# A prologue with the latent first, constant matmuls between TensorE's waits, and a second norm put in other places

## The chip, the cores and the metric

The kernel runs on one core of a Trainium2 chip. The metric is the time of one execution on the device in microseconds (us). A core has TensorE (PE, matrix products; PEld is its loading of stationary operands), VectorE (DVE), ScalarE (ACT), GpSimd (POOL) and SyncE (SP, which issues DMAs here). Each engine works through its own list of instructions in order and waits on semaphores for the others.

## The reference, cut to what matters

One layer: two token mixers (a gated linear recurrence over the sequence and a gated MLP over chunks) on a normed and modulated input, then a GEGLU MLP with a 3x3 depthwise convolution. The latent `x` has 512 tokens, the context `ctx` 256, both with 1024 channels. All arithmetic is float32.

```python
def _modulate(x, g, shift, scale):
    return _rmsnorm(x, g) * (1.0 + scale) + shift
m_x = (silu(c) @ w_mod + b_mod).reshape(B, 6, 1, D)      # for the latent
m_c = (silu(c_ctx) @ w_mod + b_mod).reshape(6, D)        # for the context
hc = _modulate(ctx, g_norm1, m_c[0], m_c[1])
pc = hc @ w_in[:, :W_R]                                  # the context needs only the columns rx
...                                                      # conv and recurrence of the context: end states
hx = _modulate(x, g_norm1, m_x[:, 0], m_x[:, 1])
px = hx @ w_in                                           # columns rx, rg, u, v, gr, gg
...                                                      # recurrence from those states, gating, merge
x = x + m_x[:, 2] * (merged @ w_out)
h2 = _modulate(x, g_norm2, m_x[:, 3], m_x[:, 4])
x = x + m_x[:, 5] * _conv_ffn(h2, w_up, ...)
return _rmsnorm(x, g_final)
```

## The kernel before, in words

Activations lie channel-major: 8 tiles of 128 channels (index k) by tokens. A float32 product is made of three passes in a rounded format: operand and weight are each split into a high part (`wh`, `hxh`: an ACT copy) and the rest (`wl`, `hxl`: a DVE subtraction), and high x high, high x low and low x high are summed in PSUM (`mm3`, L139 to L141). `Weights` (L50 to L103) hands out weight blocks in program order: `load` issues the DMA into `raw` (two buffers) on SP's queue, `prepare` splits a block, `take` returns it after preparing some blocks ahead.

The **prologue** (L214 to L350) starts every chain. In order: `c_row` and the modulation weights `wm` of block 0 are loaded, then the latent in 8 pieces, then further `wm`, the weight blocks `w_first` and the context. `sig` is silu of both conditioning rows; a transpose (`psc`) turns them into columns `c32`. `mod_cols(k)` makes shift and scale of channel block k: 16 small matmuls in four row strips into `pm`, an ACT copy `mrow`, one matmul that turns the rows into columns (`pm<-sel,mrow`), and two DVE operations into `ms`. `norm_of` squares the 8 latent blocks on ACT (L281, L284), adds them one after another on DVE (`sqs`, L285), sums over partitions with matmuls against ones (`pss`, L289), takes square root and reciprocal (`rstd_of`, L196, L197), and spreads the result over partitions (`spread_rows`, `rb`, L203). `mod_h(k, n)` applies norm and modulation to block k of the latent or the context (L328 to L330) and splits it. Then `products` (L317) multiplies block k of latent and context with six column tiles of `w_in` (rx, rg, gr) and two for the context (`rxc`); eight k-steps accumulate in PSUM. `mod_cols` and `mod_h` run two blocks ahead (`LEAD = 2`).

In the **heads** after it, `rx_head` multiplies the next rx columns while DVE makes the convolution of the head before (`pad`, `cacc`, `xr`, `xrh`, `xrl`), and `gates_head` needs its `xrl`.

Around the **second norm** (L646 to L733) the merged tokens are multiplied with `w_out`: five channel blocks over all tokens, the last three (5 to 7) in two token halves (`out_half`). `out_post` adds the residual (`x1c`, L672), squares and sums (`osq`, L677, L678). `norm2(half)` makes the statistics of one half (`qss`, `qrb`, L684 and L203) and turns its eight blocks into `h2h` and `h2l` (L694 to L697). Then the first four blocks of `w_up` (`FIRST`) run over the first half (`up_half`), blocks k 0 to 3, then `norm2` of the second half, then the rest. The two splits `wl` of each of the first two `w_up` units are made on GpSimd; two of the four pairs have buffers of their own (`extra`).

A scheduler sets each engine's order from the program, the dependencies and priorities; `after(a, b)` adds an order without a wait.

## Time and profile before

| | us |
|---|---|
| runs before, median (lowest to highest of 3) | 967.9 (967.74 to 967.97) |
| the profiled execution | 967.45 |
| its span, first to last instruction | 965.7 |
| PE busy | 938.9 (97%) |
| DVE, ACT, POOL busy | 642.5 (67%), 470.0 (49%), 41.8 (4%) |

The profiled execution lasts 1.8 us longer than its span. In the page's row of 40 slices (24.1 us each) PE reads 3 in the first slice, 8 or 9 in all others but the last, which reads 7. PE is the engine to follow: in the chain of work that ended last it has 87%. Times below count from the first instruction. A float32 matmul outside the three-pass scheme stands in the trace as two records, so 4 instructions are "x8".

### The profile page before, as it was taken

To read this page: it belongs to the slowest core of one execution; us is meant where nothing else is said; L and a number is where in the kernel's file an instruction comes from. 1 tells how busy PE (TensorE), PEld (TensorE's weight loads), DVE (VectorE), ACT (ScalarE), POOL (GpSimd) and SP (SyncE) were. 2 spreads that over 40 slices of the span, in tenths; PEclk is the share of its full clock that TensorE was granted. 3 is DMA by queue.
4 is the path that set the end of the run, shared out by engine and by line. 5 is a ranking of instruction groups with operands and counts; after the bars stand their busy time and mean duration, and the time that the engine had idled before them with its cause. 6 is when DMAs were issued, how large, how long until landed. Compare 5 with 4: busy or idle time off the path is not lost.

```text
span 965.7 us, 11855 instructions
## 1 busy us (share of the span) xinstructions
PE 938.9 (97%) x4787; PEld 791.0 (82%) x4787; DVE 642.5 (67%) x863; ACT 470.0 (49%) x639; POOL 41.8 (4%) x69
## 2 busy tenths in 40 slices
PE   3999999999999999999999998999999999999997
PEld 3788888888888788888888888988888888888886
DVE  3667595969493886555773547598885437788644
ACT  4536969794989681233332334254333122333323
POOL 0000000000000011000200112000000000000020
PEclk9999999999999999999999999999999999999999
DMA  9542122122131266622853531122212232222222
GB/s 354 213 163 88 44 88 75 57 88 94 61 114 61 85 224 239 235 88 88 315 212 121 203 126 49 61 97 98 94 66 88 101 140 87 88 88 88 88 88 88
DMA packets 23511, 116.85 MB, mean 121 GB/s; under 512 B 2576, under 2 KB 3744, under 8 KB 14368
## 3 DMA queue, kind: packets, MB, share of 16 engines
q1 hardware_dynamic: 17488, 94.59, 27.3%
q0 software_dynamic: 5968, 21.50, 6.2%
q8 instruction: 37, 0.61, 0.3%
q14 instruction: 18, 0.15, 0.0%
HBM read 113.98 MB, written 2.10 MB: 120 GB/s over the span
## 4 chain that ended last, share of the span: by engine, by line
PE 87%; DVE 5%; ACT 5%; issue 1%; DMA 1%; SPq 0%; DVEq 0%; ACTq 0%
PE up L139 8%; PE up L141 8%; PE up L140 8%; PE d L140 4%; PE d L141 4%; PE d L139 4%; PE pr L139 2%; PE pr L140 2%; PE pr L141 2%; PE u L139 2%; PE u L140 2%; PE u L141 2%; PE gg L140 2%; PE pg L139 2%; PE gg L139 2%; PE pg L140 2%
## 5 line engine op out<-in xcount | busy, mean ns | idle before, releaser
L93 ACT CAST wh<-raw 128x1024 fp32r<-128x1024 f32 (+1 forms) x156 | 161.9, 1040 | 299.9 <-PE up L140 79.6
L95 DVE TENSOR_TENSOR wl<-raw,wh 128x1024 fp32r<-128x1024 f32 (+1 forms) x152 | 184.2, 1214 | 153.0 <-ACT wh L93 136.1
L139 PE MATMUL up<-h2h,wh 128*128 128x512 f32 (+1 forms) x384 | 143.8, 374 | 0.0
L141 PE MATMUL up<-h2h,wl 128*128 128x512 f32 (+1 forms) x384 | 143.5, 374 | 0.0
L140 PE MATMUL up<-h2l,wh 128*128 128x512 f32 (+1 forms) x384 | 143.2, 373 | 0.0
L792 DVE SCALAR_TENSOR_TENSOR acc<-up,sm,acc 128x441 f32<-128x441 f32 (+2 forms) x176 | 120.2, 693 | 14.2 <-ACT acc L785 10.4
L141 PEld LDWEIGHTS up<-h2h,wl 128*128 128x128 f32 x384 | 73.0, 190 | 12.4
L139 PEld LDWEIGHTS up<-h2h,wh 128*128 128x128 f32 x384 | 73.0, 190 | 12.3
L140 PEld LDWEIGHTS up<-h2l,wh 128*128 128x128 f32 x384 | 73.0, 190 | 12.3
L140 PE MATMUL d<-wl,fh 128*128 128x512 f32 (+1 forms) x186 | 70.3, 378 | 0.0
L139 PE MATMUL d<-wh,fh 128*128 128x512 f32 (+1 forms) x186 | 70.3, 378 | 0.0
L141 PE MATMUL d<-wh,fl 128*128 128x512 f32 (+1 forms) x186 | 70.3, 378 | 0.0
L795 ACT ACTIVATE acc<-acc 128x512 f32<-128x512 f32 x22 | 13.9, 632 | 61.4 <-DVE acc L792 61.4
L558 DVE SCALAR_TENSOR_TENSOR wmod<-wmod,cbx 128x1024 f32<-128x1024 f32 x24 | 29.3, 1223 | 17.7 <-DMA wmod<-in_w_mod 17.7
L139 PEld LDWEIGHTS d<-wh,fh 128*128 128x128 f32 x186 | 35.0, 188 | 6.6
L140 PEld LDWEIGHTS d<-wl,fh 128*128 128x128 f32 x186 | 35.0, 188 | 6.5
L141 PEld LDWEIGHTS d<-wh,fl 128*128 128x128 f32 x186 | 35.0, 188 | 6.4
L474 DVE TENSOR_TENSOR i<-i,xr 128x768 f32<-128x768 f32 x20 | 18.9, 954 | 19.6 <-ACT i L467 19.6
L140 PE MATMUL g<-xrl,wh 128*128 128x512 f32 x80 | 31.5, 394 | 0.0
L139 PE MATMUL g<-xrh,wh 128*128 128x512 f32 x80 | 31.5, 394 | 0.0
L141 PE MATMUL g<-xrh,wl 128*128 128x512 f32 x80 | 31.2, 390 | 0.0
L141 PE MATMUL pr<-yrh,wl 128*128 128x512 f32 x80 | 31.2, 389 | 0.0
(314 smaller groups left out, 2106.4 us busy)
## 6 DMA issues: line engine op xcount, KB each, us to landing
raw<-in_w_up SPq DMA_DIRECT2D x22, 1024.0 KB, 4.7
wmod<-in_w_mod POOLq DMA_DIRECT2D x32, 512.0 KB, 4.9
raw<-in_w_down SPq DMA_DIRECT2D x22, 512.0 KB, 3.2
wm<-in_w_mod SPq DMA_DIRECT2D x8, 1024.0 KB, 8.5
raw<-in_w_lru SPq DMA_DIRECT2D x5, 1024.0 KB, 4.8
raw<-in_w_pr SPq DMA_DIRECT2D x5, 1024.0 KB, 6.3
raw<-in_w_rx SPq DMA_DIRECT2D x4, 1024.0 KB, 4.7
raw<-in_w_rg SPq DMA_DIRECT2D x4, 1024.0 KB, 4.8
```

What stands on the lines that cost most here:

```text
L93: nc.scalar.copy(h[:, :n], r)
L95: eng.tensor_tensor(l[:, :n], r, h[:, :n].bitcast(F32), op=ALU.subtract)
L139: nc.tensor.matmul(o, wh, xh, start=first, stop=False)
L140: nc.tensor.matmul(o, wh, xl, start=False, stop=False)
L141: nc.tensor.matmul(o, wl, xh, start=False, stop=last)
L474: nc.vector.tensor_tensor(i[u], i[u], xr[h][:, u % 2, :], op=ALU.mult)
L558: nc.vector.scalar_tensor_tensor(wm, wm, 1.0, cbx, op0=ALU.mult, op1=ALU.mult, accum_out=m)
L792: nc.vector.scalar_tensor_tensor(o, g3[:, r0 + dy : r1 + dy, c0 + dx : c1 + dx], col("ffw", 9 * i + q), o, op0=ALU.mult, op1=ALU.add)
L795: nc.scalar.activation(accf, accf, AF.Gelu_apprx_tanh)
```

## The change

1. **Loads.** The latent comes first, in 4 pieces of two blocks (`xin`), before `wm0`; the first two weight blocks get loads of their own; the context (`cin`) comes behind the fourth `wm`; `c_b` moves from GpSimd's queue to SP's, behind the last weights. `W.queued` chains all these DMAs in program order. `wm` has three buffers instead of four.
2. **Constant matmuls.** `idle(n)` multiplies `ident` by `ones`, both 128x128 float32, into an unread PSUM tile: 15 around the transpose, one between the groups of sums, 6 before the first products. `in_line` orders all of TensorE's matmuls up to there.
3. **Sums.** Square 7 is made on DVE; only squares 0 to 3 and 6 to 7 are added there; the matmuls against ones take four partial sums and accumulate in PSUM. The square root's table is loaded right after the sigmoid's (`root`).
4. **Blocks.** `LEAD` is 1: in step k the first column tile's products stand first, then `mod_cols(k+1)`, then the rest. All split weights of the eight steps are kept (`whl1`, 8 buffers). The context's norm follows step 4, its products all stand behind the eighth step. `c_b`'s sigmoid, the exponential of `lam` and the gates gr come after that.
5. **Second norm.** `norm2` is cut into `sums2` (statistics) and `norm2` (application); the first half is applied behind `out_half` of the second; the second half's statistics come after k = 0 to 2 and are applied after k = 7 in program order. All four pairs of `FIRST` have own buffers, all splits are on DVE, casts after them wait behind the last `h2h` in order. `x1c` is loaded in 4 pieces.

```diff
-LEAD = 2
+LEAD = 1
+WARM = 15
+CTX_AT = 3
...
+    for k in range(2):
+        W.add(a["w_first"][0][:, k * FW : (k + 1) * FW], [FW], extra=True)
+    for i in range(1, 4):
+        W.add(a["w_first"][i], [FW] * 2, extra=True)
...
-            add_tiles("w_up", i, on_pool=i <= 1, extra=i == 0)
+            add_tiles("w_up", i, extra=i <= 1)
...
+        for i in range(4):
+            W.queued(nc.sync.dma_start(xin[:, 2 * i : 2 * i + 2, :].rearrange("p k t -> p (k t)"), a["xc"][i]))
         load_mod(0)
+        W.queued(nc.sync.dma_start(sm, a["smalls"]))
+        W.load(0)
         load_mod(1)
+        W.load(1)
         load_mod(2)
...
+        def idle(n):
+            for _ in range(n):
+                in_line(nc.tensor.matmul(warm[:, :P], ident, ones, start=True, stop=True))
+        idle(WARM // 3)
+        in_line(nc.tensor.transpose(psc[:, : 2 * KD], sig, ident[: 2 * KD, : 2 * KD]))
+        idle(WARM - WARM // 3)
...
+        for k in range(KD - 1):
+            after(nc.scalar.activation(sqs[k], xin[:, k, :], AF.Square), rooted)
+        for k in range(1, 4):
+            add = nc.vector.tensor_tensor(sqs[0], sqs[0], sqs[k], op=ALU.add)
...
+        add = after(nc.vector.tensor_tensor(sqs[7], xin[:, 7, :], xin[:, 7, :], op=ALU.mult), add)
+        add = nc.vector.tensor_tensor(sqs[6], sqs[6], sqs[7], op=ALU.add)
+        for k in (0, 4, 5, 6):
+            for t in range(4):
+                in_line(nc.tensor.matmul(pss[:, t : t + 1], sqs[k][:, t * P : (t + 1) * P], ones1,
+                                         start=k == 0 and t == 0, stop=k == 6 and t == 3))
+            if k != 6:
+                idle(1)
+        r = rstd_of(pro, pss[:, :4], "n1x", 4)
...
+        pm, rows, turn = mod_strips(0, in_line)
+        for t in range(4):
+            in_line(nc.tensor.matmul(prb[:, t * P : (t + 1) * P], r[:, t : t + 1].to_broadcast([P, P]), ident,
+                                     start=True, stop=True))
+            if t == 1:
+                in_line(mod_turn(0, pm, rows))
+        idle(6)
...
+            mm = products(k, *blks[k], OUTS[:1])
+            if k + 1 < KD:
+                mod_cols(k + 1, mm)
+                mod_h(k + 1, 0)
+            last = products(k, *blks[k], OUTS[1:])
+            if k == CTX_AT + 1:
+                cprb = norm_sums("c", cin, TC, TC // P)
...
+        for k in range(KD):
+            products(k, *blks[k], COUTS)
...
         out_half(*HALVES[0])
-        norm2(*HALVES[0])
+        rb = sums2(*HALVES[0])
         out_half(*HALVES[1])
+        norm2(rb, *HALVES[0])
...
-        up_half(*HALVES[0], range(KD // 2))
-        norm2(*HALVES[1])
-        up_half(*HALVES[0], range(KD // 2, KD))
+        up_half(*HALVES[0], range(3))
+        rb = sums2(*HALVES[1])
+        up_half(*HALVES[0], range(3, KD))
+        norm2(rb, *HALVES[1])
         up_half(*HALVES[1], range(KD))
```

TensorE's list from the program's start, before. `pm` are the modulation strips, `pss` the sums against ones, `rb` the spread, `rx` the first product.

```order
L244 MATMUL psc<-ident,sig 128x16
L265 MATMUL pm_136<-wm_97,c_123 32x128 x16
L269 MATMUL pm_136<-sel,mrow_153 128x4
L289 MATMUL pss_181<-ones,sqs 128x1 x4
L203 MATMUL rb_189<-ident,n1256r 128x128 x4
L265 MATMUL pm_195<-wm_109,c_123 32x128 x16
L269 MATMUL pm_195<-sel,mrow_212 128x4
L317 MATMUL rx_253<-hxh,wh_257 128x512
```

The same list now (`warm` are the constant matmuls, `pssx` the four groups of sums, `rbx` the spread):

```order
L279 MATMUL warm<-ones,ident 128x128 x5
L283 MATMUL psc<-ident,sig 128x16
L279 MATMUL warm<-ones,ident 128x128 x10
L364 MATMUL pssx<-ones,sqx_148 128x1 x4
L279 MATMUL warm<-ones,ident 128x128
L364 MATMUL pssx<-ones,sqx_152 128x1 x4
L279 MATMUL warm<-ones,ident 128x128
L364 MATMUL pssx<-ones,sqx_153 128x1 x4
L279 MATMUL warm<-ones,ident 128x128
L364 MATMUL pssx<-ones,sqx_154 128x1 x4
L303 MATMUL pm_192<-wm_106,c_122 32x128 x16
L373 MATMUL rbx<-ident,n1xr 128x128 x2
```

Behind these rows stand the turn of `pm`, two more `rbx`, six `warm` and the first product; the strips of block 1 moved from before the first product to behind the sixth.

SP's list from the start, before (`xc` is the latent, then the context; `raw` are weights):

```order
L218 DMA crow<-in_c_row 16x128
L223 DMA wm_97<-in_w_mod 128x2048
L228 DMA xc<-in_xc 128x512 x8
L229 DMA sm<-in_smalls 128x402
L223 DMA wm_109<-in_w_mod 128x2048
L80 DMA raw_111<-in_w_first 128x1536
L223 DMA wm_113<-in_w_mod 128x2048
L233 DMA xc<-in_ctx 128x8x256
```

And now:

```order
L241 DMA crow<-in_c_row 16x128
L251 DMA xin<-in_xc 128x1024 x4
L246 DMA wm_106<-in_w_mod 128x2048
L253 DMA sm<-in_smalls 128x402
L93 DMA raw_109<-in_w_first 128x768
L246 DMA wm_111<-in_w_mod 128x2048
L93 DMA raw_113<-in_w_first 128x768
L246 DMA wm_115<-in_w_mod 128x2048
```

The latent moved ahead of the first 1 MB of modulation weights, and the context out of these rows.

DVE's list at the first half's statistics of the second norm, before (the three `x1c` of 256 tokens are blocks 5 to 7 of the first half, `wl` a weight split):

```order
L95 TENSOR_TENSOR wl_4460<-raw_4424,wh_4459 128x1024
L678 TENSOR_TENSOR sqs<-sqs,osq_4455 128x512
L672 SCALAR_TENSOR_TENSOR x1c<-o_4458,mcol,x1c 128x256
L678 TENSOR_TENSOR sqs<-sqs,osq_4500 128x256
L672 SCALAR_TENSOR_TENSOR x1c<-o_4463,mcol,x1c 128x256
L678 TENSOR_TENSOR sqs<-sqs,osq_4528 128x256
L672 SCALAR_TENSOR_TENSOR x1c<-o_4470,mcol,x1c 128x256
L678 TENSOR_TENSOR sqs<-sqs,osq_4556 128x256
L197 RECIPROCAL n2r<-n2r 128x2
```

And now:

```order
L111 TENSOR_TENSOR wl_4494<-raw_4458,wh_4493 128x1024
L789 TENSOR_TENSOR sqs<-sqs,osq_4489 128x512
L783 SCALAR_TENSOR_TENSOR x1c<-o_4492,mcol,x1c 128x256
L789 TENSOR_TENSOR sqs<-sqs,osq_4544 128x256
L111 TENSOR_TENSOR wl_4512<-raw_4509,wh_4511 128x1024
L111 TENSOR_TENSOR wl_4516<-raw_4509,wh_4515 128x1024
L783 SCALAR_TENSOR_TENSOR x1c<-o_4497,mcol,x1c 128x256
L783 SCALAR_TENSOR_TENSOR x1c<-o_4508,mcol,x1c 128x256
L789 TENSOR_TENSOR sqs<-sqs,osq_4572 128x256
L789 TENSOR_TENSOR sqs<-sqs,osq_4600 128x256
L218 RECIPROCAL n2r<-n2r 128x2
```

Two weight splits, which GpSimd made before, now stand on DVE ahead of blocks 6 and 7.

## Rows read from the trace of the kernel before

**Rows 1.** The page's first section: busy us, share of the span, instructions.
```profile
PE 938.9 (97%) x4787; PEld 791.0 (82%) x4787; DVE 642.5 (67%) x863; ACT 470.0 (49%) x639; POOL 41.8 (4%) x69
```

**Rows 2.** Timeline of PE, 0 to 30: start, us, operation, [idle before, releaser].
```profile
10.25 1.93 PE L265 MATMUL pm<-wm,c 128*32 128x128 f32 x32 [6.95 <-DVE c L245]
...
14.94 1.87 PE L289 MATMUL pss<-ones,sqs 128*128 128x1 f32 x8 [1.72 <-DVE sqs L285]
18.71 2.08 PE L203 MATMUL rb<-ident,n1256r 128*128 128x128 f32 x8 [1.91 <-DVE n1256r L197]
```

**Rows 3.** Windows: us, busy of PE, PEld, DVE, ACT, POOL (count), clock, DMA, GB/s.
```profile
5.00:10.00 5.00, 0.00 (x0) 0.00 (x0) 0.58 (x1) 1.84 (x3) 0.00 (x0) 1.00 1.02 402
24.08:28.70 4.62, 4.57 (x22) 2.93 (x26) 3.35 (x5) 1.31 (x2) 0.00 (x0) 0.63 1.02 425
24.08:76.37 52.29, 51.78 (x405) 40.66 (x405) 34.33 (x79) 27.10 (x50) 0.25 (x6) 0.97 0.47 180
76.37:93.05 16.68, 16.68 (x99) 14.77 (x97) 13.59 (x17) 7.49 (x12) 0.00 (x0) 1.00 0.28 106
594.83:602.20 7.37, 4.73 (x26) 4.65 (x27) 4.03 (x11) 2.36 (x6) 0.00 (x0) 0.77 0.00 0
588.91:617.42 28.51, 25.86 (x202) 25.58 (x201) 14.62 (x34) 8.63 (x19) 1.01 (x1) 0.94 0.11 37
```

**Rows 4.** Timeline of PE, 37 to 41: the same kinds of matmul later.
```profile
37.39 0.60 PE L289 MATMUL pss<-ones,sqs 128*128 128x1 f32 x4
37.85 0.48 PE L317 MATMUL rx<-hxh,wl 128*128 128x512 f32 x1
...
39.47 1.07 PE L265 MATMUL pm<-wm,c 128*32 128x128 f32 x30
```

**Rows 5.** Timeline of all engines, 0 to 24: the latent's chain on ACT and DVE.
```profile
7.41 0.63 ACT L281 ACTIVATE sqs<-xc 128x512 f32<-128x512 f32 x1 [4.82 <-DMA xc<-in_xc]
...
10.22 3.88 DVE L285 TENSOR_TENSOR sqs<-sqs,sq 128x512 f32<-128x512 f32 x5
...
21.45 0.75 DVE L328 SCALAR_TENSOR_TENSOR xc<-xc,ms,rb 128x512 f32<-128x512 f32 x1 [2.79 <-ACT rb L294]
...
22.58 0.72 ACT L329 ACTIVATE hxh<-xc,ms 128x512 fp32r<-128x512 f32 x1
```

**Rows 6.** DMA issues 1.0 to 6.3: KB each, median us to landing.
```profile
wm<-in_w_mod SPq DMA_DIRECT2D x1, 1024.0 KB, 4.9
cbx<-in_c_b POOLq DMA_DIRECT2D x1, 512.0 KB, 6.7
```

**Rows 7.** Timeline of PE, 590 to 606: the wait at the second half's statistics.
```profile
597.47 0.58 PE L684 MATMUL qss<-ones,sqs 128*128 128x1 f32 x4 [2.65 <-DVE sqs L678]
```

**Rows 8.** Timeline of all engines, 60 to 64.5: modulation of block 7.
```profile
60.52 1.08 PE L265 MATMUL pm<-wm,c 128*32 128x128 f32 x32
...
63.71 0.72 ACT L329 ACTIVATE hxh<-xc,ms 128x512 fp32r<-128x512 f32 x1 [1.72 <-DVE xc L328]
```

**Rows 9.** Timeline of DVE, 560 to 640: around the second norm.
```profile
566.06 1.23 DVE L95 TENSOR_TENSOR wl<-raw,wh 128x1024 fp32r<-128x1024 f32 x1
567.20 0.68 DVE L678 TENSOR_TENSOR sqs<-sqs,osq 128x512 f32<-128x512 f32 x1
...
579.23 0.48 DVE L672 SCALAR_TENSOR_TENSOR x1c<-o,mcol,x1c 128x256 f32<-128x256 f32 x1 [1.44 <-PE o L141]
...
583.04 1.67 DVE L694 SCALAR_TENSOR_TENSOR h<-x1c,mcol,rb 128x256 f32<-128x256 f32 x4 [1.21 <-ACT rb L690]
...
585.02 5.57 DVE L697 SCALAR_TENSOR_TENSOR h2l<-h,mcol,h2h 128x256 fp32r<-128x256 f32 x4
...
591.71 1.26 DVE L697 SCALAR_TENSOR_TENSOR h2l<-h,mcol,h2h 128x256 fp32r<-128x256 f32 x3
...
595.89 0.47 DVE L672 SCALAR_TENSOR_TENSOR x1c<-o,mcol,x1c 128x256 f32<-128x256 f32 x1
```

More of the change, by code (lines that the diff above doesn't have):

```diff
@@ L60, in __init__ @@
         self.boost = 0
+        self.behind = self.last = None
+        self.chain = None
         self.units = []
@@ L90, in prepare @@
             hl = self.extra if extra else self.hl
-            h = hl.tile([P, BLK], F32R, tag="wh", name=f"wh{self.split}")
-            l = hl.tile([P, BLK], F32R, tag="wl", name=f"wl{self.split}")
-            nc.scalar.copy(h[:, :n], r)
+            w = n if extra else BLK
+            h = hl.tile([P, w], F32R, tag="wh", name=f"wh{self.split}")
+            l = hl.tile([P, w], F32R, tag="wl", name=f"wl{self.split}")
+            cast = nc.scalar.copy(h[:, :n], r)
+            if self.behind is not None:
+                self.behind(cast)
             eng = nc.gpsimd if on_pool else nc.vector
@@ L277, in hybrid_block @@
[L277 to L287 removed]
+            return pm, rows, nc.scalar.copy(rows, pm[:, :P])
@@ new lines, in mod_turn @@
+        def mod_turn(k, pm, rows):
+            mm = nc.tensor.matmul(pm[:, P : P + 4], rows, sel.rearrange("p s n -> p (s n)"), start=True, stop=True)
+            ms = mss[k] = pro.tile([P, 2, 2], F32, tag="ms", name=f"ms{k}", bufs=KD)
+            nc.vector.tensor_scalar(ms[:, :, 1], pm[:, P + 2 : P + 4], bm1[:, k : k + 1], col("g1", k),
+                                    op0=ALU.add, op1=ALU.mult)
+            nc.vector.tensor_scalar(ms[:, :, 0], pm[:, P : P + 2], col("bmod", k), None, op0=ALU.add)
+            return mm
@@ new lines, in mod_cols, with order, norm_sums @@
+        def mod_cols(k, behind):
+            first = []
+            def order(mm):
+                if not first:
+                    after(mm, behind)
+                first.append(mm)
+            mod_turn(k, *mod_strips(k, order)[:2])
+        rb = pro.tile([P, TT], F32, name="rb")
+        ones1 = ones[:, 0:1]
+        def norm_sums(name, x, r0, n):
+            sqs = pro.tile([P, T], F32, tag="sqs", name=f"sqs{name}")[:, :r0]
+            gate = lambda k: hxs[CTX_AT + 1 + k // 4]
+            after(nc.scalar.activation(sqs, x[:, 0, :], AF.Square), gate(0))
+            for k in range(1, KD):
+                q = pro.tile([P, T], F32, tag="sq", name=f"sq{name}{k}", bufs=4)[:, :r0]
+                after(nc.scalar.activation(q, x[:, k, :], AF.Square), gate(k))
+                nc.vector.tensor_tensor(sqs, sqs, q, op=ALU.add)
+            pss = aux_tile(f"pss{name}", 0)
@@ new lines, in hybrid_block @@
+        after(nc.scalar.copy(rb[:, TC:], prb), hxs[1])
+        blks, ready = [], 0
+        for k in range(KD):
+            blks.append(W.take(ahead=1 if k < KD - 1 else 0))
+            if k == 0:
+                W.load(2)
+            elif k == 2:
+                W.load(3)
+            elif k == 3:
+                W.load(4)
+                W.queued(nc.sync.dma_start(cbx, a["c_b"]))
+            if k + 3 < KD:
+                load_mod(k + 3)
+            if k == 0:
+                W.queued(nc.sync.dma_start(cin.rearrange("p k t -> p (k t)"), a["ctx"]))
+            mm = products(k, *blks[k], OUTS[:1])
[5 more added lines that the diff above has]
+                cprb = norm_sums("c", cin, TC, TC // P)
+                normed = nc.scalar.copy(rb[:, :TC], cprb)
+            if k > CTX_AT + 1:
+                for _ in range(3):
+                    if ready < KD:
+                        mod_h(ready, 1)
+                        ready += 1
@@ L350, in hybrid_block @@
+        rxc = aux_tile("rxc", 0)
+        COUTS = [(rxc[:, j * TC : (j + 1) * TC], j, 1) for j in range(2)]
+        for k in range(KD):
+            products(k, *blks[k], COUTS)
+        after(starts["c"], last)
+        for j in range(2):
+            rx_ps[j] = (rx_ps[j], COUTS[j][0])
+        W.prepare(KD + 1)
+        W.chain = W.behind = None
+    exp.close()
     W.boost = 1000
-    nc.gpsimd.dma_start(cbx, a["c_b"])
+    amp, am_pool = opened("am")
+    am = am_pool.tile([P, KD, T], F32, name="am")
```

183 lines of the change are left out of this document (87 added, 96 removed).

## The prediction

> **What bounds the kernel now.** I read the page's busy times first, then the timeline of PE, then windows over the stretches where PE does little. PE is busy 97% of the span [rows 1], so a change can win time only where PE stands still or runs slowly. There are two such places. The first is the start: PE has only short bursts, between waits of 7.0, 1.7 and 1.9 us [rows 2]; its first large product begins at 24.08, and even then the granted clock reads 0.63 up to 28.70 [rows 3]. The bursts themselves ran at about half the rate that the same kinds reach later: the eight `pss` records took 1.87 us, while four of them at 37.39 let the next matmul start 0.46 us later; the 32 strip records took 1.93 us, and 30 of them took 1.07 later [rows 2, 4]. (The clock column reads 1.00 there, so for that stretch I go by durations.) The second place is the statistics of the second norm's second half: between 594.83 and 602.20 PE is busy 4.73 of 7.37 us at a clock of 0.77 [rows 3]. The change addresses both. Everything else on PE keeps its work, and nearly its order.
>
> **Part 1, up to the first product.** I follow the new order with the old durations.
> *Loads.* The first square began at 7.41, when the first latent piece had landed [rows 5], behind 1.05 MB of `wm`. At 402 GB/s [rows 3] that megabyte costs 2.6 us; without it a first piece lands at about 4.8. The new pieces are twice as large (0.65 us more), but the 512 KB of `c_b`, which came in between on GpSimd's queue [rows 6], are gone too; I let these cancel. Pieces then follow at 0.52 MB / 402 GB/s = 1.3 us: 4.8, 6.1, 7.4, 8.7. `wm0` lands 2.6 us later, at 11.3, and the first weights 1.5 us after that. All of these come down one queue. Before, `wm` was issued at about 1.2 and landed 4.9 us later [rows 6], the first latent piece, issued behind it, 1.3 us after that; so I count on issue order.
> The Trainium skill (DMA: Bandwidth & Descriptors, Queues, rings and completion order) speaks against that: completion is not first in, first out per issuing engine, because a copy is spread over many rings. If the last latent piece therefore landed only with `wm0`, at 11.3, its sums would be there at 12.8 and the first product 0.9 us later than below; the rows bear out issue order within SP's queue.
> *Sums.* Squares take 0.63 us each and the dependent adds 0.78 [rows 5]. Squares 2 and 3 end near 7.3, so the sum of 0 to 3 is there at 8.3. Square 6 and, on DVE, square 7 start at 8.7; with one add they are there at 10.2. Before, seven adds in a row stood here.
> *TensorE's fixed order.* A group of four sums costs 1.87 us at the slow rate and 0.93 at the fast one. A constant matmul has no row of its own; the nearest are the `rb` records, also 128 columns: 2.08/8 x 2 = 0.52 us slow [rows 2], half of it, 0.26, fast. The `ident` tile is there at about 1.6, an estimate on which nothing hangs below. Five constants and the transpose last until 4.5. When does the rate double? In both rises that rows show, PE had worked without a wait since 24.08 (597.47), and the slow stretch ended at 28.70 (602.20) [rows 3, 7]. I put the rise as far behind the first constant, at 6.2; the bounds are "never before the products" (the first rival) and at once. So three or four more constants are slow, the rest fast, and the 15 end at 7.9, before the first sum. Then PE itself is the bound: four groups and three constants, 4 x 0.93 + 3 x 0.26 = 4.5 us, from 8.35 to 12.85. The strips of block 0 (1.0) end at 13.85; root and reciprocal of four columns run beside them. `mrow`, the turn and the four spreads end at 15.0; the multiplication takes 0.75 and `hxh` 0.72 [rows 5]. With hand-overs of about 0.1 us the **first product starts at 16.6 instead of 24.08**: 7.5 us. The table load for the square root, once between `pss` and the root, hides behind the first DMA wait. Casts and splits of block 0 fit beside the spreads, since its weights land at 12.8.
>
> **Part 2, the eight steps.** From 24.08 to the heads at 76.37 pass 52.29 us, PE busy 51.78 [rows 3]. Away go the slow rate (1.7 us by the clock of 0.63, 2.3 by half of 4.57 busy; I take 2.0) and 0.5 idle. One more block of strips and its turn comes in, 1.3. The context products only move to the end. The lead of one block instead of two may add waits: block k+1's strips follow three to six products of step k, and from their start to the end of `hxh` pass 3.9 us (60.52 to 64.43) [rows 8]. What covers this on PE is the strips and turn, 1.3, and 12 to 15 products at 0.23 (72 such units in 16.68 us [rows 3]): 4.1 to 4.75. So 0 to 0.2 us at a boundary, and something where the context's squares stand ahead of `mrow` on ACT: 0.7 in all. 52.3 - 2.0 - 0.5 + 1.3 + 0.7 = 51.8, and the heads start at 68.4: **8.0 us gained so far**. DMA is no bound: a step needs 1.44 MB, 3.6 us, and lasts 5.9; loads that wait for a buffer on SP wait for work a step or more ahead of their use.
>
> **Part 3, heads.** The convolution of head 0 needs the context products, which now come last. Its cover is head 1's products, 16.68 us, in which DVE was busy 13.59 [rows 3]. It stays covered, by 3.1 us: no gain or loss. Sigmoids and `c_b` moved around it are ACT work beside PE: nothing.
>
> **Part 4, second norm.** From 588.91 to 617.42 pass 28.51 us [rows 3]. The work is 192 products of 256 columns at 0.12 and eight small records, 24.1 us. The 4.4 us between them are the 2.65 us wait [rows 7] and the slow stretch behind it (7.37 x 0.23 = 1.7). The wait came because `x1c` of block 7 ended on DVE only at 596.4, 7 us after its product: four `h2l` had taken 5.57 us, where three take 1.26 at other times [rows 9], with splits running on GpSimd. Now GpSimd makes none. DVE then has 16 operations of 0.42 (1.67/4, 1.26/3) and five more for the sums from 583.0 on and is through at about 592; PE has 36 products, 4.3 us, to 593.2. The statistics cost no wait, with a margin of 1 us, and 60 products (7.2 us) cover the second half's first blocks.
> The price lies before: two splits now stand ahead of blocks 6 and 7 of the first half. `w_up` unit 1 can load when unit 0 is split. DVE now does that behind the add that ends at 567.9: two splits of 1.23, 570.3. It lands 4.9 later at 575.2, is cast twice (1.05) and split twice by 578.9; with `x1c` of block 6 that is 579.4, where block 7's `x1c` started at 579.23 [rows 9]. A margin of nothing; I take off 0.2. **Gain 4.2.**
>
> **Sum.** Against the profiled execution: 967.45 - 8.0 - 4.2 = 955.25. That execution lies 0.45 under the median of the runs, so the predicted median is **955.7**.
>
> **The rivals.**
> *The clock does not come, or goes again* (0.20). In the first 24 us PE had matmuls of these kinds and stayed slow. Against it: those were bursts of 2 us at most between waits, now 15 stand back to back. Slow throughout, the fixed order is the bound: 4.5 + 5.2, then 4 x 1.87 + 3 x 0.52 = 9.0, strips 1.9, spreads and turn 2.3, then 1.7: first product at 24.6, and the 2.0 of the slow products return, so the heads start at 78.4, 2.0 late: 967.9 + 2.0 - 4.2 = 965.7. Half of it, a rate that rises only between the groups, gives about 960.
> The Trainium skill (TensorE: Matmul & The Clock Gate, A second HAM failure mode: psum-queue depth-cycling) describes short idle times between groups of matmuls that let the clock swing between its levels. The groups of sums with one moving column are such a place; if it fell at the first group, the product would start near 23.3 and the time be about 964. The row that bears on this is the burst of `pss` at 14.94, slow after a wait of 1.72 us [rows 2], though PE had not been fast before it.
> *The lead of one block is too short* (0.09). Place: the seven boundaries of the eight steps; mechanism: strips, `mrow`, turn, `ms`, multiplication and `hxh` pass through ACT's and DVE's queues, which in steps 3 to 7 also carry the context's squares, adds and 24 modulations. With a wait of 1 us each the time is 962. It eats the whole gain at 12.2/7 = 1.75 us, and from 2.0 us (a chain of over 6 us instead of 3.9) the kernel is slower than before: 970 or more. For it speaks the doubled dependence, against it that DVE is busy 34 and ACT 27 of 52 us [rows 3]. 0.05 of it for slower.
> *The wait of the second norm moves to the first half* (0.07): if unit 1 lands as late as before, splits end 2 us later, PE waits 2 us and slows down: 4.2 shrinks to 0.5, 959.4.
> *Head 0 gives some back* (0.05): if `lam`'s small operations fall into DVE's 13.6 us too and ACT is late, 1 to 3 us: 957 to 958.7.
>
> **How the numbers follow.** Forecast, 953 to 957.7: 0.55. Faster than that, if the sums are quicker: 0.04. With half of the clock rival, the second norm's and head 0's cases, the range 952 to 962 holds about 0.8. A measurement here can tell about 0.2%, 1.9 us: under 966.0 lie all cases but the worst clock and the short lead. Faster 0.91, same 0.04, slower 0.05.
>
> **What would show it.** First product near 16.6; `pss` groups of 0.93 us; strips of 1.0; clock 1.00 from the first product on; heads at 68.4; `qss` of the second half without a wait and 24 us from the first `up` product of 256 columns to the first of 512. Wrong it is if groups take 1.87 us, if PE waits for `hxh` at each step, or if the first `qss` waits for DVE.

## The result, and the profile after

The changed kernel takes 958.4 us (median of four runs: 958.28, 958.40, 958.41 and 960.93) against 967.9 before (967.74 to 969.02): a ratio of 0.9904, 95% interval 0.9892 to 0.9916. The run of 960.93 left no trace; its mean granted clock was 0.998, that of the other three 0.995. The forecast was 955.7 with a range of 952 to 962: the direction and the range held, and 2.7 us of the expected 12.2 are missing. PE's share of the span rose from 97% [rows 1] to 99%, and GpSimd's busy time fell by 12.6 us:

```profile
PE 945.2 (99%) x4859; PEld 797.7 (83%) x4859; DVE 642.4 (67%) x864; ACT 470.9 (49%) x639; POOL 29.2 (3%) x60
```

The timeline of PE from the wait for `sig` to the first product (start, us, operation, count of records, idle time before):

```profile
4.62 0.28 PE L283 MATMUL psc<-ident,sig 16*128 16x16 f32 x1 [0.65 <-DVE sig L264]
4.83 4.25 PE L279 MATMUL warm<-ones,ident 128*128 128x128 f32 x20
8.92 0.95 PE L364 MATMUL pssx<-ones,sqx 128*128 128x1 f32 x8
...
11.98 0.78 PE L279 MATMUL warm<-ones,ident 128*128 128x128 f32 x2
12.55 1.71 PE L364 MATMUL pssx<-ones,sqx 128*128 128x1 f32 x8
14.18 1.93 PE L303 MATMUL pm<-wm,c 128*32 128x128 f32 x32
16.05 1.22 PE L373 MATMUL rbx<-ident,n1xr 128*128 128x128 f32 x4
...
20.14 0.73 PE L395 MATMUL rx<-hxh,wh 128*128 128x512 f32 x2
```

The waits of [rows 2] are gone, and `pssx` groups of 0.95 us show the full rate that the forecast wanted. But the last group took 1.71, the strips 1.93 instead of 1.0, and four `rbx` records 1.22. Windows over the same stretches, and over the steps and the second norm (us, busy of PE, PEld, DVE, ACT, POOL, clock, DMA share, GB/s), show where the rate went down:

```profile
8.50:11.90 3.40, 3.40 (x33) 3.40 (x32) 1.38 (x2) 1.58 (x3) 0.00 (x0) 1.00 0.99 403
11.98:18.77 6.79, 6.79 (x57) 6.29 (x56) 0.94 (x5) 1.26 (x3) 0.00 (x0) 0.50 0.94 390
20.14:70.51 50.37, 50.37 (x439) 39.82 (x439) 35.35 (x75) 26.64 (x49) 0.32 (x6) 1.00 0.64 246
584.00:608.10 24.10, 24.10 (x202) 23.98 (x201) 13.17 (x29) 9.71 (x19) 0.00 (x0) 1.00 0.13 45
```

From 11.98 to 18.77 the granted clock was 0.50, the 1.2 GHz level, with PE busy without a gap before the fall and throughout. The products then ran at 1.00 from the first on. Laid against the windows of [rows 3], the time went so:

| stretch | before | after | gain | forecast |
|---|---|---|---|---|
| start to first product | 24.08 | 20.14 | 3.94 | 7.5 |
| eight steps, to the heads | 52.29 | 50.37 | 1.92 | 0.5 |
| heads to the first `up` product of 256 columns | 512.54 | 513.49 | -0.95 | 0 |
| from there to the first of 512 columns | 28.51 | 24.10 | 4.41 | 4.2 |
| rest of the span | 348.3 | 348.3 | 0 | 0 |
| sum | | | 9.3 | 12.2 |

Two lines are off by more than a microsecond, the first by 3.5 us of loss and the second by 1.4 of gain, and in the heads something new costs 0.95. In the list of PE's waits (total us, times, longest) it stands here; before the change there was one such wait, of 0.8:

```profile
PE gc L155 <- ACT r L581: 1.7, 2, 0.9
```

The second norm went as forecast. On DVE (timeline) the two new splits and the last blocks of both halves:

```profile
571.03 2.36 DVE L111 TENSOR_TENSOR wl<-raw,wh 128x1024 fp32r<-128x1024 f32 x2 [1.02 <-ACT wh L107]
...
575.35 0.43 DVE L789 TENSOR_TENSOR sqs<-sqs,osq 128x256 f32<-128x256 f32 x1 [0.21 <-ACT osq L788]
...
585.65 0.43 DVE L789 TENSOR_TENSOR sqs<-sqs,osq 128x256 f32<-128x256 f32 x1
```

and on PE the statistics of both halves, without a wait:

```profile
575.83 0.61 PE L795 MATMUL qss<-ones,sqs 128*128 128x1 f32 x4
...
588.32 0.50 PE L795 MATMUL qss<-ones,sqs 128*128 128x1 f32 x4
```

The first half's last add ends at 575.78, 0.05 us ahead of its reader; the second half's at 586.08, 2.2 ahead.

### The profile page after: what moved, and what is told of

Its sections match the earlier page's. It is cut to its first block, busy times and chain, and to the rows that moved or that the text cites. A ratio compares the mean times of both kernels' runs of the same rounds, so it can differ in the third digit from the quotient of the medians.

```text
span 956.4 us, 11976 instructions
## 1 busy us (share of the span) xinstructions
PE 945.2 (99%) x4859; PEld 797.7 (83%) x4859; DVE 642.4 (67%) x864; ACT 470.9 (49%) x639; POOL 29.2 (3%) x60
## 4 chain that ended last, share of the span: by engine, by line
PE 86%; ACT 8%; DVE 4%; issue 1%; DMA 0%; ACTq 0%; DVEq 0%
PE up L155 8%; PE up L156 8%; PE up L157 8%; PE d L155 4%; PE d L156 4%; PE d L157 4%; PE pr L156 2%; PE pr L155 2%; PE pr L157 2%; PE o L156 2%; PE o L155 2%; PE o L157 2%; PE u L156 2%; PE u L155 2%; PE u L157 2%; PE gg L156 2%
## 5 line engine op out<-in xcount | busy, mean ns | idle before, releaser
L111 DVE TENSOR_TENSOR wl<-raw,wh 128x1024 fp32r<-128x1024 f32 (+1 forms) x156 | 188.0, 1208 | 146.9 <-ACT wh L107 132.1
L157 PEld LDWEIGHTS up<-h2h,wl 128*128 128x128 f32 x384 | 72.3, 188 | 12.6
L156 PEld LDWEIGHTS up<-h2l,wh 128*128 128x128 f32 x384 | 72.4, 188 | 12.2
L155 PE MATMUL pr<-yrh,wh 128*128 128x512 f32 x80 | 31.1, 389 | 0.0
L156 PE MATMUL pr<-yrl,wh 128*128 128x512 f32 x80 | 31.1, 389 | 0.0
```

What stands on the lines that cost most here:

```text
L111: eng.tensor_tensor(l[:, :n], r, h[:, :n].bitcast(F32), op=ALU.subtract)
L155: nc.tensor.matmul(o, wh, xh, start=first, stop=False)
L156: nc.tensor.matmul(o, wh, xl, start=False, stop=False)
L157: nc.tensor.matmul(o, wl, xh, start=False, stop=last)
```

## Experiments: the rate at the start

The theory was that the rate fell because of what PE ran there, groups of sums that move one column. The rival was that it goes down some time after it rose, whatever runs.

**All 128 columns.** The sums move the whole block of ones:

```diff
-in_line(nc.tensor.matmul(pss[:, t : t + 1], sqs[k][:, t * P : (t + 1) * P], ones1,
+in_line(nc.tensor.matmul(pss[:, t * P : (t + 1) * P], sqs[k][:, t * P : (t + 1) * P], ones,
...
-r = rstd_of(pro, pss[:, :4], "n1x", 4)
+r = rstd_of(pro, pss.rearrange("p (t c) -> p t c", c=P)[:, :, 0], "n1x", 4)
```

> The changed kernel, but each of the 16 sums over partitions takes the 128-column block of ones as its moving tile instead of one column of it (every column of the result then holds the sum, and the first is used). In the changed kernel a one-column record and a 128-column record both follow one another at 0.112 us at the full rate, so PE's time for the groups should not change. Theory A (the granted clock fell at 11.9 because of what PE ran there, three groups of one moving column): the clock stays at 1.00 from 8.5 on, the last group takes 0.9 instead of 1.7, the strips 1.05 instead of 1.9, each pair of spreads 0.6 instead of 1.2; the stretch from 11.98 to 18.77 shrinks by some 3.2 us, the first product starts at 16.8 to 17.0 and the time is about 955.2. Rival B (the rate goes down a while after it rose, whatever runs): first product at 20.1 and 958.4, with the clock at 0.50 from about 12 to 19.

PE's timeline:

```profile
8.62 1.06 PE L364 MATMUL pssx<-ones,sqx 128*128 128x128 f32 x8
...
11.97 1.06 PE L364 MATMUL pssx<-ones,sqx 128*128 128x128 f32 x8
12.96 1.08 PE L303 MATMUL pm<-wm,c 128*32 128x128 f32 x32
...
17.02 0.73 PE L395 MATMUL rx<-hxh,wh 128*128 128x512 f32 x2 [0.26 <-ACT hxh L416]
```

Groups follow one another at the same distance as one-column groups at the full rate (1.11 us with their constant), the strips take 1.08, and the first product starts at 17.02. Measured: 956.2 us (955.41 to 956.53), mean clock 0.998 to 0.999 in all four runs, where it was 0.995 in three of the changed kernel's four. That is theory A, with a time 1 us above the one expected.

**No constants.**

```diff
 def idle(n):
-    for _ in range(n):
+    for _ in range(0):
```

> The changed kernel without any constant matmul (none before the transposition, behind it, between the groups or before the first product); the output does not depend on them. Theory: the four groups then start with the first sum at 8.0 and run at the half rate throughout, 1.71 each, to 14.9; strips 1.9 to 16.7, spreads and turn 2.3 to 19.0, the first product 1.8 later at about 20.8, and the products start at the half rate, which costs 2.0 to 2.3 more as before the change: 958.4 + 0.7 + 2.1 = about 961.2. If the constants are worth nothing: 958.4. If they are worth what the prediction put on them (first product at 24.6 without): 964 or more.

```profile
8.26 6.99 PE L364 MATMUL pssx<-ones,sqx 128*128 128x1 f32 x32 [3.18 <-DVE sqx L355]
...
21.13 1.22 PE L395 MATMUL rx<-hxh,wh 128*128 128x512 f32 x2 [1.59 <-ACT hxh L416]
```

Measured: 962.4 in one run, 1.2 above the time expected. Slow throughout as expected (two products 1.22 instead of 0.73; the clock column first changes at 24.83), and the steps last 53.40 instead of 50.37, of which two more waits for `hxh` are 1.0. By this run the constants are worth 4.0 us to the changed kernel although the rate falls again.

**Three constants between the groups** instead of one, sums of one column:

```diff
-                idle(1)
+                idle(3)
```

> The changed kernel (one-column sums) with three constants between the groups instead of one: 6 x 0.224 = 1.3 us more for PE at the full rate. If more constants keep the rate up, the first product starts at 16.8 + 1.3 = 18.1 with the clock at 1.00 to the first product, 2 us earlier than in the changed kernel, and the time is 956.5. If it falls anyway it starts at 20.1 + 1.5 to 2 = 21.6 to 22 and the time is about 960.

```profile
18.12 0.73 PE L395 MATMUL rx<-hxh,wh 128*128 128x512 f32 x2 [0.25 <-ACT hxh L416]
```

The rate stayed and the first product came where it was expected, at 18.12. The time was 959.0 all the same: PE waited 1.17 us at 393.7 and 0.33 at 494 for weight splits that it waits for in no trace of the changed kernel, and the steps took 51.0. This is one run, and what delayed those splits stays open.

**The changed kernel again**, four more runs, unaltered.

> The changed kernel once more, unaltered. Three runs of it and the old-order run had a mean clock of 0.995 and a fall at 12; the run with GpSimd's splits, whose first 20 us are the same instructions, had none (mean clock 0.998, first product at 16.77 as forecast). Theory A (with one-column groups it depends on how the groups happen to lie in time whether the rate falls): both clocks occur among the runs, those of 0.995 some 3 us longer than those of 0.998, as the spans show. Theory B (the changed kernel always falls and the GpSimd run was different for another reason): all runs at 0.995 and 958.4. The wide runs beside it should show 0.998 or 0.999 every time by either.

```profile
12.99 1.26 PE L364 MATMUL pssx<-ones,sqx 128*128 128x1 f32 x8
```

958.9 us (958.3 to 959.31), clock 0.994 or 0.995 each time. By the distance of the records the rate rose here inside the first group, at about 10.1, and fell inside the last, at about 13.5, so neither instant is tied to an instruction. With the four runs of the result, the run with the old order and the one with GpSimd's splits (both below; the first 20 us of all are the same instructions), there are ten runs of one-column sums with one constant between. Eight read 0.994 or 0.995, and the three of them that have a trace show the fall. Two read 0.998: the run with GpSimd's splits, whose trace shows no fall, and the run of 960.93, which was slower by 2.5 us all the same. A mean clock of 0.998 alone does not show a fast start: the run without constants reads it too. Of the five wide versions in which PE waits at most 1.5 us in one place at the start, all 17 runs read 0.998 or 0.999, and none of their five traces shows a fall, also where the rate rose as late as 9.7 and 10.1. So A is borne out as a matter of frequency, and B, a fall whatever runs, is out. Why the run with GpSimd's splits escaped stays open; its trace shows the earliest rise, at 7.6, with seven records of constants left at the full rate ahead of the first sum, where the three traces that fell have three, one and none (rises at 8.5, 8.9 and 10.1).

**Wide and tight**: wide sums, no constant between them.

```diff
-            if k != 6:
-                idle(1)
```

> The wide sums of the first run (128 moving columns) and, besides, no constant matmul between the four groups. In the wide run the groups began at 8.62, 9.74, 10.85 and 11.97, each a constant pair later than PE could; the last sum of squares was there at 10.9. Without the three constants the third group ends at 11.3 and the last at 12.2, the strips at 13.25 (the first modulation weights land at about 12), spreads and turn at 14.5, the first product at 16.2 instead of 17.0: 0.7 to 0.8 us less than the wide run, 955.4 if that stands at 956.2. Rival: the three constants were what kept the rate up; then the clock reads 0.50 somewhere from 12 to 19 and the first product is at 19 to 20.

```profile
9.25 4.12 PE L364 MATMUL pssx<-ones,sqx 128*128 128x128 f32 x32
...
17.36 0.73 PE L393 MATMUL rx<-hxh,wh 128*128 128x512 f32 x2 [0.26 <-ACT hxh L414]
```

955.2 us (954.67 to 955.74), 0.9863 (0.9847 to 0.988) of before, clock 0.998 to 0.999. With wide sums the constants between groups are not needed. In the profiled run the rate rose only inside the first group, at about 10.1, so the product came at 17.36 and not at 16.2; in the version with the early sigmoid, below, the same code had it at 16.53.

## Experiments: loads, sums and the transposition

All on the wide, tight version. **Weights first:**

```diff
+        load_mod(0)
         for i in range(4):
             W.queued(nc.sync.dma_start(xin[:, 2 * i : 2 * i + 2, :] ...
-        load_mod(0)
```

> The wide, tight version with the first modulation weights (1 MB) issued ahead of the latent again. By the prediction's step the latent's four pieces land 2.6 us later (7.0, 8.4, 10.9, 12.1 instead of 4.4, 5.8, 8.3, 9.5), the last sum of squares is there at 13.5, the last group ends at 14.6, and the first product starts 2.3 to 2.6 later than in the tight version (18.6): about 2.4 us slower than it. Rival (the order of the loads is hidden, since PE's own list bounds the start): the same first product within 0.5.

```profile
10.96 5.18 PE L364 MATMUL pssx<-ones,sqx 128*128 128x128 f32 x32 [1.42 <-DVE sqx L355]
...
20.13 0.73 PE L393 MATMUL rx<-hxh,wh 128*128 128x512 f32 x2 [0.26 <-ACT hxh L414]
```

958.4 in one run: the first product 2.77 later, 3.2 us on the time. Not all of it is the megabyte. The latent's four pieces landed 1.9 to 2.2 later than in the tight version (7.41, 8.67, 9.92 and 11.16 against 5.18, 6.49, 7.99 and 9.21), and the first group starts 1.7 later (10.96 against 9.25). The other 1.1 is the rate: by the distance of the records it rose only at about 13.8, and the groups took 5.18 instead of 4.12.

**One group:** all seven adds in a row, one group of sums.

```diff
-        add = nc.vector.tensor_tensor(sqs[6], sqs[6], sqs[7], op=ALU.add)
+        for k in (4, 5, 6, 7):
+            add = nc.vector.tensor_tensor(sqs[0], sqs[0], sqs[k], op=ALU.add)
...
-        for k in (0, 4, 5, 6):
+        for k in (0,):
```

> The wide, tight version with all seven adds of squares in a row on DVE and one group of sums over partitions instead of four, as before the change. DVE then adds block 4 after 8.3, 5 and 6 after 9.5, and the last sum is there at about 11.9 instead of 11.0; one group takes 0.9. Theory (the prediction's step: the chain of adds cost time): if PE were free it would end at 12.8 against 13.3 measured with four groups, so no gain of the groups is left, but PE stands still from about 9.3 to 11.9 and the rate may fall, which costs up to 3: between 0.5 us faster and 3 us slower than the tight version. A rival that groups save 2 us or more by themselves would show a last group ending at 15 with the rate at 1.00.

```profile
12.54 2.08 PE L365 MATMUL pssx<-ones,sqx 128*128 128x128 f32 x8 [3.72 <-DVE sqx L360]
14.55 1.94 PE L303 MATMUL pm<-wm,c 128*32 128x128 f32 x32
```

958.6 in one run. The last sum is 1.7 us later than in the tight version, but behind the wait of 3.72 us the rate is down: the group takes 2.0, the strips 1.94, and the first product starts at 20.23. At the full rate the group would have ended at 13.4, an estimate from its start at 12.54 and 0.9 for eight records, against 12.5 to 13.3 with four. By that the groups' own saving is 0.1 to 0.9 us; the larger part of their worth is that PE does not stand still.

**Transposition last**, with 20 constants ahead of it (and the early sigmoid of the next section):

```diff
-        idle(WARM // 3)
+        idle(WARM)
         in_line(nc.tensor.transpose(psc[:, : 2 * KD], sig, ident[: 2 * KD, : 2 * KD]))
-        idle(WARM - WARM // 3)
```

> As the run with the early sigmoid, and the transposition of the silu column stands behind all constants instead of behind a third of them; there are 20 constants instead of 15, so that PE runs from 1.47 without the wait of 0.64 us. Theory A (the rate rises a while after PE last stood still): it rises before 6 instead of at 8.4 to 9.6, the 20 constants end near 7.7, the groups start with the first sum at about 8.0 and run at the full rate, the last waits for its sum (11.1) and ends at 12.0, the first product starts at 16.0 to 16.3 instead of 17.36: 1.1 to 1.4 less. Rival B (the rise does not depend on that wait): 20 slow constants last to 10, the groups end at 13.6 to 14, first product at 17.5 to 18: 0.3 to 0.6 more.

```profile
1.46 6.08 PE L279 MATMUL warm<-ones,ident 128*128 128x128 f32 x40 [1.46 <-POOL eps L211]
...
10.30 5.47 PE L363 MATMUL pssx<-ones,sqx 128*128 128x128 f32 x32 [2.60 <-DVE sqx L354]
```

957.6 (956.9 to 958.2): slower, and neither theory's time. By the distance of the records the rate rose at about 4.3 and 40 records took 6.08 us, so theory A's rise came. But DVE's timeline shows what I had left out:

```profile
7.81 0.17 DVE L284 COPY c<-psc 128x16 f32<-128x16 f32 x1 [3.25 <-PE psc L283]
7.98 2.27 DVE L354 TENSOR_TENSOR sqx<-sqx,sqx 128x512 f32<-128x512 f32 x3
```

The adds stand behind the copies of the transposed column on DVE, and moved back with them: the first sum came at 10.3 instead of 8.0, and PE waited 2.60 us. Behind that wait the records lie 0.112 us apart for another 0.9 us; then the rate fell at 11.16, to a granted clock of 0.50 until 14.57. So in this run wide sums did not keep the rate behind the wait.

## Experiments: the second norm and the heads

**Splits on GpSimd again**, the new order kept:

```diff
-            add_tiles("w_up", i, extra=i <= 1)
+            add_tiles("w_up", i, on_pool=i <= 1, extra=i <= 1)
```

> The changed kernel, but the four weight splits of the first two w_up units are made by GpSimd again, as before the change; the new order of the second norm stays. Theory (the wait came because DVE runs slowly while GpSimd splits): a DVE operation of 0.42 us takes up to 1.4 us while GpSimd splits, the second half's last square sum comes later, and the four one-column matmuls of its statistics wait 1 to 2.6 us; with the slow stretch behind it 1.5 to 4.4 us of the 4.4 gained here go: 960 to 962.8. Rival (the order of the code does it): 958.4, no wait.

GpSimd's timeline and DVE's:

```profile
570.24 2.40 POOL L111 TENSOR_TENSOR wl<-raw,wh 128x1024 fp32r<-128x1024 f32 x1 [6.01 <-ACT wh L107]
...
572.59 2.53 POOL L111 TENSOR_TENSOR wl<-raw,wh 128x1024 fp32r<-128x1024 f32 x1
```

```profile
571.46 1.46 DVE L789 TENSOR_TENSOR sqs<-sqs,osq 128x256 f32<-128x256 f32 x1 [2.95 <-ACT osq L788]
572.85 0.47 DVE L783 SCALAR_TENSOR_TENSOR x1c<-o,mcol,x1c 128x256 f32<-128x256 f32 x1
573.86 1.54 DVE L789 TENSOR_TENSOR sqs<-sqs,osq 128x256 f32<-128x256 f32 x1 [0.54 <-ACT osq L788]
```

and PE's, at the start and at the first half's statistics:

```profile
16.77 0.73 PE L395 MATMUL rx<-hxh,wh 128*128 128x512 f32 x2 [0.26 <-ACT hxh L416]
```

```profile
575.46 0.61 PE L795 MATMUL qss<-ones,sqs 128*128 128x1 f32 x4 [3.03 <-DVE sqs L789]
```

958.0 in one run, with a rate that happened to stay at the start (first product at 16.77). Against its own first product the stretch from the first `up` product of 256 columns on begins 3.0 us later than in the changed kernel. While GpSimd splits, DVE's adds take 1.46 and 1.54 us instead of 0.43; the operation between them, one of whose tensors lies in PSUM, takes its usual 0.47. The theory's mechanism is shown, and the two adds' excess, 2.1 us, is the larger part of the wait; its place was not the second half but the first, which the prediction's third rival had named for another cause. The Trainium skill (VectorE: DVE Perf Modes, Two Vector instructions with no wait between them) says that an instruction with two tensor inputs in SBUF reads the second through an interface shared with GpSimd; these three rows agree.

The ends of the rows say more than their lengths. The adds end at 572.92 and 575.40, each 0.28 us behind the GpSimd split that was running when it began (572.64 and 575.12). By these ends an add is not slowed by a factor but held until the running split has ended. The kernel before shows the same in the four `h2l` that took 5.57 us [rows 9]:

```profile
584.36 2.63 POOL L95 TENSOR_TENSOR wl<-raw,wh 128x1024 fp32r<-128x1024 f32 x1 [11.84 <-DVE h L694]
```

```profile
585.02 2.24 DVE L697 SCALAR_TENSOR_TENSOR h2l<-h,mcol,h2h 128x256 fp32r<-128x256 f32 x1
```

This one ends at 587.26, again 0.28 behind the split. The third ends at 590.20, 0.28 behind the next split's end at 589.92. The second and the fourth began while no split ran and took 0.47.

**Old order, splits on DVE:**

```diff
         rb = sums2(*HALVES[0])
-        out_half(*HALVES[1])
         norm2(rb, *HALVES[0])
+        out_half(*HALVES[1])
...
-        up_half(*HALVES[0], range(3))
+        up_half(*HALVES[0], range(4))
         rb = sums2(*HALVES[1])
-        up_half(*HALVES[0], range(3, KD))
         norm2(rb, *HALVES[1])
+        up_half(*HALVES[0], range(4, KD))
```

> The changed kernel with the second norm written in the old order (the first half's modulation ahead of the second half of the out products; four of eight blocks of the first up half ahead of the second half's statistics), the splits on DVE as in the change. Theory (GpSimd's splits were the cause, the order adds little): 958.4 within 0.5 us, no wait before the second half's statistics. Rival (the order does it): the wait of 2.65 us and the slow stretch behind it come back, 962.8.

958.45. The window from the first `up` product of 256 columns to the first of 512, in the columns shown above:

```profile
584.18:608.26 24.08, 24.08 (x202) 23.96 (x201) 13.17 (x29) 9.36 (x19) 0.00 (x0) 1.00 0.13 45
```

24.08 against 24.10, in one run: with the splits on DVE the new order adds nothing here.

**`lam` early**, on the wide, tight version. Its operations moved from the heads into the third step:

```diff
             last = products(k, *blks[k], OUTS[1:])
+            if k == 2:
+                lam = col("lam", 0, 20)
...
-        after(nc.vector.scalar_tensor_tensor(z, lam, -1.0, lam, op0=ALU.mult, op1=ALU.max), inverse["n1c"])
+        nc.vector.scalar_tensor_tensor(z, lam, -1.0, lam, op0=ALU.mult, op1=ALU.max)
```

> The wide, tight version with the 17 small operations on lam (some 3.5 us of DVE from 65 to 73.5 in the changed kernel) moved from the heads into the third of the eight steps. Theory (the new wait of 0.85 us at the second head's gates comes from DVE being busy longer at head 0: 15.40 of 16.68 us against 13.59 before the change, which delays the sigmoids' buffers): one of the two waits of PE for ACT at the gates goes, and the time is 0.8 below the tight version. Rival (the order on ACT at the first gates makes it): two waits and the same time.

```profile
12.22 0.18 DVE L450 SCALAR_TENSOR_TENSOR z<-sm 128x20 f32<-128x20 f32 x1 [2.23 <-DMA sm<-in_smalls]
12.32 0.69 DVE L359 TENSOR_TENSOR sqx<-sqx,sqx 128x512 f32<-128x512 f32 x1
```

958.6 (957.87 to 959.54), slower by 3.4 than the tight version, which was not expected: the scheduler put the first operation ahead of the last add of squares, which then stood behind the landing of `sm`. For the question it was put to it still answers: with DVE relieved in head 0 (busy 14.31 us of its first 16.68 instead of 15.36), PE's two waits at the gates remain, 1.7 us as before. DVE's load was not the cause.

**A sigmoid ahead.** In the changed kernel the ACT timeline at head 0's gates, and the gelu that waits a head later:

```profile
88.61 1.28 ACT L580 ACT_TABLE_LOAD   x1
89.90 0.69 ACT L580 ACTIVATE r<-g,sm 128x512 f32<-128x512 f32 x1
...
133.48 0.60 ACT L559 ACTIVATE rgs<-rg 128x512 f32<-128x512 f32 x1 [0.88 <-DVE yr L606]
```

and in the kernel before, where no load stands ahead of the same sigmoid:

```profile
94.64 0.69 ACT L466 ACTIVATE r<-g,sm 128x512 f32<-128x512 f32 x1 [0.18 <-PE g L141]
```

Against the start of the heads the sigmoid starts at 18.27 before and at 19.39 after. The edit, on the wide, tight version:

```diff
-            nc.scalar.activation(rgs[j], rg_ps.pop(j), AF.Gelu_apprx_tanh)
+            gelu = nc.scalar.activation(rgs[j], rg_ps.pop(j), AF.Gelu_apprx_tanh)
+            if j == 1:
+                after(nc.scalar.activation(lru.tile([P, 1], F32, name="sigt"), ones[:, 0:1], AF.Sigmoid), gelu)
```

> The wide, tight version with one more ACT operation: a sigmoid of one column right behind head 0's two gelus. In the changed kernel the gate sigmoids of the first 512-column blocks moved ahead of the gelus, so that head 0's gates have to load the sigmoid table first, 1.28 us at 88.61 with PE's results already there; before the change the gelus came first and no load stood there. Theory: this load delays ACT and DVE through head 0 and head 1 (the first head's output was multiplied 1.9 us later against the start of the heads than before the change), and a gelu of head 1 then waits for its buffer, and the second head's gates for ACT, 0.85 us. With the load done in ACT's idle time the list of PE's waits has one wait for ACT at the gates instead of two, and the time is 0.8 us below the tight version (954.4 if that stands at 955.2). Rival: two waits remain, same time.

PE's start and its list of waits:

```profile
8.70 3.84 PE L364 MATMUL pssx<-ones,sqx 128*128 128x128 f32 x32
...
16.53 0.73 PE L393 MATMUL rx<-hxh,wh 128*128 128x512 f32 x2 [0.25 <-ACT hxh L414]
```

```profile
PE pr L157 <- DVE wl L111: 0.9, 1, 0.9
PE gc L155 <- ACT r L581: 0.8, 1, 0.8
```

The sigmoid is back at 18.28 and one of the two waits is gone, as expected. The run with the transposition last has the same sigmoid, and its list too has one wait of 0.8 at the gates. 954.5 us (954.14 to 955.18), 0.7 below the tight version, though the two sets of runs overlap; 0.9844 (0.9814 to 0.9874) of the kernel before, whose runs beside it spread from 967.5 to 972.3. That the 0.7 come from the sigmoid is not shown. In the profiled run, the slowest of the four, a wait of 0.86 us for a weight split at 390.6 takes the gain back: from the start of the heads to the first `up` product of 256 columns pass 513.96 us, in the tight version's trace 513.47. What this trace gains is its earlier first product. The run with the transposition last, without that wait, needs 512.82 for the stretch; by that the sigmoid is worth 0.65. The wait for the split stands also in the runs with three constants and with `lam` early, and its cause stays open. This version beats both kernels.

## Why the prediction was right, and where it was not

*What bounds the kernel.* Right: all that was won came from the two places named, the start with the steps behind it and the second norm, and PE's busy share is 99%.

*The loads.* The latent's pieces landed at 4.45, 5.80, 8.28 and 9.52 and `wm0` at 11.99, in issue order as assumed, the third and fourth 0.9 late; the last sum came at 11.1 instead of 10.2. It cost nothing, since PE's own list was the bound. The megabyte was put at 2.6 and measured 1.9 to 2.2 in the landings; that the first product moved by 2.77 with the weights first is a coincidence, since 1.1 of it is the rate.

*The rise of the rate.* Put at 6.2, measured at 8.5. Constants cost less than assumed, 0.43 and 0.22 us instead of 0.52 and 0.26, which made up for part of it: they ended at 8.9 instead of 7.9.

*The groups: the step that failed.* "Four groups and three constants, 4.5 us, from 8.35 to 12.85", with the rate taken as granted once it had risen. Where it stayed, the step was right: in the run with GpSimd's splits the last group ended at 12.7 and the first product started at 16.77, forecast 16.6. In the changed kernel the rate was down for 6.79 us, half of them lost, 3.4 us; the first product came at 20.14. This is the first rival, a clock that goes again, but in neither of the places that I had priced: 960 for a rate that rises only between the groups, 964 for one that falls at the first group. The kernel came out between the forecast and 960 because the steps gave 1.4 more than forecast, for reasons that are not in the forecast; to that extent the small miss is luck. The Trainium skill (TensorE: Matmul & The Clock Gate, A second HAM failure mode: psum-queue depth-cycling) has such swings come from short idle times between groups of matmuls. The fall at the groups agrees, the idle times do not, as far as the profile can tell: PE was busy 3.40 of 3.40 us ahead of the fall, though the ends of matmuls are modelled, so that idle time inside a record would not show.

The trace of before held a warning that I read over. The clock of 0.63 in [rows 3] is a mean of two levels:

```profile
24.08:25.30 1.22, 1.17 (x4) 0.69 (x5) 1.22 (x3) 1.22 (x2) 0.00 (x0) 1.00 1.03 426
25.30:28.70 3.40, 3.40 (x19) 2.23 (x22) 2.13 (x3) 0.09 (x1) 0.00 (x0) 0.50 1.02 424
```

The first large product ran at the full rate, which by the distance of the records had come at 21.9, and the rate fell at 25.30 with PE at work. The second norm's 0.77 is the same: 1.00 up to 598.7, then 0.50 to 602.15. So "In the first 24 us PE had matmuls of these kinds and stayed slow" was not right, and a rate that rises and falls again with PE at work could have been read there.

*The eight steps.* 0.5 forecast, 1.92 measured. Of the price of 0.7 for the lead of one block nothing came: PE is busy 50.37 of 50.37 us, so the second rival is out. The extra block was the other error. Adding the time from each record's start to the next one's, strips and turns take 8.34 instead of 7.87, 0.47 more, where I had put 1.3: a block costs less where all of them run at the full rate. The products of the latent give 1.07, where the sum had 2.5 for the slow rate and the idle time of the whole stretch. That shortfall, of which a part lies in the strips, was made up by gains the sum did not have: the context's products, now in one row, 0.95, their statistics another 0.4.

*The heads.* "Sigmoids and `c_b` moved around it are ACT work beside PE: nothing." That was wrong by a table load. The cover of head 0 did hold, against its own rival, but the load delayed a chain that only a head later made PE wait.

*The second norm.* 4.2 forecast, 4.41 measured. The mechanism was right: the splits on DVE alone remove the wait, in the old order too. The margin in the second half, put at 1 us, is 2.2. The price in the first half, a margin of nothing, was read closely: 0.05 us are left there. With GpSimd's splits a wait does move there (3.03), to the third rival's place, but the cause is the held adds and not a unit that lands late; the rival's own cause was not tested.

## To carry to other kernels

A stretch that is to run at TensorE's full rate has to be looked at in the clock column to its end, not only at its rise: here the rate went down again with PE busy all the time, in 8 of 10 runs, and sums that move 128 columns instead of one cost PE the same and kept it wherever PE did not wait long ahead of them. A mean of the clock over a window can hide such a fall, as the 0.63 did. Where an operation is moved on ACT, write down which function table is loaded before and after each place; a load of 1.28 us can show up as a wait on PE a whole head later. And where an operation is moved back in a fixed order, everything queued behind its readers moves with it, as the adds did behind the transposed column.

## What the runs showed of the hardware that I had not expected

- A float32 sum with one moving column and one with 128 follow the record before them at the same distance, 0.112 us at the full rate; at the half rate one-column records and constants both take 0.213.
- The clock column reads 1.00 from the start although in the changed kernel's profile records lie 0.213 apart until 8.5 and 0.112 afterwards; it tells the rate only from its first change on.
- The rise of the rate moved between 7.6 and 10.1 from run to run with the same instructions ahead of it; it came at 13.8 in the run with the weights first and at 4.3 in the one run where PE did not stand still from 1.46 on.
- A DVE operation of 128x256 on two SBUF tensors that begins while a GpSimd split runs ends 0.28 us behind that split, in two of two adds and two of two `h2l`; an operation that reads one tensor from PSUM takes its usual 0.47 beside it.
